# One-word key selection, with the larger tile compared in bfloat16 on VectorE and its ones summed by ScalarE

## The chip, the cores and the metric

One core of one Trainium2 chip runs one inference step of a small decoder: two layers, a prompt of 1024 tokens and a group of 8 x 8 sampled tokens. The metric is the device time of one execution in microseconds (us), the median over the runs shown. Engines are named as in the profile: PE is TensorE, DVE is VectorE, ACT is ScalarE, POOL is GpSimd, SP is SyncE.

## What is computed

Layer 0 is an RWKV-7 mixer, layer 1 an attention whose keys are chosen by an indexer; each is followed by a feed-forward block. The change lies in the choice of keys of layer 1. For each query the 256 best scored keys are kept:

```
score = einsum('bths,bth->bts', relu(logits), wi)        # 8 index heads, added up with weights
adm   = pos_k <= pos_q
_, idx = top_k(where(adm, score, -inf), 256)             # ties: the lower position first
o     = softmax over the 256 chosen keys only, then the values
```

The kernel doesn't sort. It finds, for every query (one query per partition), the 256th largest score as a threshold, by bisection over the 31 bits below the sign, and then turns the row of scores into a mask that is added to the attention logits.

## The kernel before, in words

The prompt is split in group A (64 sampled tokens and 512 prompt tokens) and group B (512 prompt tokens). Most of the work is a float32 product split in three matmuls of high and low parts (`mm3`, line 140); its inputs are weights that SP loads, ACT rounds (line 122, `wh`), and POOL or DVE subtracts (line 126, `wl`). Results are added to the residual stream by DVE (lines 388, 392, 394, tiles `xr` and `rt`).

Attention of A is written in `att_mixed`, of B in `att_prompt`. In both, Python generators are advanced in turn by `together`, one step of each per round, and a share of a step of a background generator (`side`: the output projection and feed-forward block of the other group) is drawn per round at a rate from a table. The tile framework then sets the final order on each engine: it lists the instructions by readiness under its own estimates of their length, so the order on PE, DVE and ACT moves wherever these estimates move. Each engine takes its own list strictly in order.

A tile of prompt queries has its scores computed by `att_post` (lines 1140 to 1151: matmuls `ip`, ACT's `rl`, DVE's sum into `sc`), its threshold found by `topk`, and is then attended in `att_tile` (line 1264: logits plus mask, DVE; line 1268: exponential, ACT; lines 1285 to 1291: transposes and values, PE). `topk` runs four times:

- on tiles 3 and 4 of A together (384 and 512 keys), beside tiles 1 and 2 of A and the index scores of the sampled tokens;
- on the sampled tokens alone (64 partitions, 2056 keys), beside tiles 3 and 4 of A;
- on tiles 0 and 1 of B together (640 and 768 keys), beside the scores of tiles 2 and 3;
- on tiles 2 and 3 of B together (896 and 1024 keys), beside tiles 0 and 1.

Everything in `topk` is on DVE. Line 1190 copies the upper halves of the float32 words to bfloat16 tiles `tu`. Line 1197 (`count`) compares a row with a threshold per partition and adds up the ones in the same instruction (`accum_out`, which shows as a second instruction, a read of the accumulator). Per bit there are six instructions for a pair of tiles and five for the sampled tokens: line 1204 sets the bit in the candidate (`tcand`), line 1205 turns it into a float (`tcf`, for negative thresholds with all bits flipped by `txm`), line 1197 counts each tile (from `tu` for bits 30 to 16, from `sc` below), line 1207 asks whether 256 or more passed (`tok`), and line 1208 keeps the candidate where so (`tm`). After the last bit one more count gives the number above the threshold, and lines 1224 to 1232 make the mask.

Of the kernel before, what the change touches and what calls it, by code (L numbers as in the profile page):

```python
# [9 lines left out]
F32 = mybir.dt.float32  # L10
F32R = mybir.dt.float32r
F16 = mybir.dt.float16
I32 = mybir.dt.int32
BF16 = mybir.dt.bfloat16
AF = mybir.ActivationFunctionType
ALU = mybir.AluOpType
# [9 lines left out]
TOPK = 256  # L26
# [51 lines left out]
class Kern:  # L78
# [1092 lines left out]
    def topk(self, pp, scs, R=128, place={}, order=None):  # L1171

        nc = self.nc
        n = len(scs)
        def T1(nm, shape, dt=F32):
            tag, bufs = place.get(nm, (nm, 1))
            return pp.tile(shape, dt, name=nm, tag=tag, bufs=bufs)
        Lm = max(s.shape[1] for s in scs)
        cnt = T1("cnt", [128, n])[0:R]
        m = T1("tm", [128, n], I32)[0:R]  # L1180
        cand = T1("tcand", [128, n], I32)[0:R]
        cf = T1("tcf", [128, n], I32)[0:R]
        xm = T1("txm", [128, n], I32)[0:R]
        ok = T1("tok", [128, n], I32)[0:R]
        junk = T1("tj", [128, Lm], BF16)[0:R]

        ups = []
        for i, s in enumerate(scs):
            u = T1("tu%d" % i, [128, Lm], BF16)[0:R, 0:s.shape[1]]
            nc.vector.tensor_copy(u, s.bitcast(BF16).rearrange("p (l b) -> p l b", b=2)[:, :, 1])  # L1190
            ups.append(u)
        yield

        def count(th, op, src):
            for i, s in enumerate(src):
                L = s.shape[1]
                nc.vector.tensor_scalar(out=junk[:, 0:L], in0=s, scalar1=th if isinstance(th, float) else th[:, i:i + 1], scalar2=None,
                                        op0=op, op1=ALU.add, accum_out=cnt[:, i:i + 1])
        count(0.0, ALU.is_ge, scs)
        nc.vector.tensor_scalar(out=xm, in0=cnt, scalar1=float(TOPK) - 0.5, scalar2=-1.0, op0=ALU.is_lt, op1=ALU.mult)  # L1200
        nc.vector.memset(m, 0)
        yield
        for b in range(30, -1, -1):
            nc.vector.tensor_scalar(out=cand, in0=m, scalar1=1 << b, scalar2=None, op0=ALU.bitwise_or)
            nc.vector.tensor_tensor(out=cf, in0=cand, in1=xm, op=ALU.bitwise_xor)
            count(cf.bitcast(F32), ALU.is_ge, ups if b >= 16 else scs)
            nc.vector.tensor_scalar(out=ok, in0=cnt, scalar1=float(TOPK) - 0.5, scalar2=None, op0=ALU.is_ge)
            nc.vector.copy_predicated(m, ok, cand)
            yield
        nc.vector.tensor_tensor(out=cf, in0=m, in1=xm, op=ALU.bitwise_xor)  # L1210
        th = cf.bitcast(F32)
        count(th, ALU.is_gt, scs)
        yield
        for i, s in enumerate(scs):
            L = s.shape[1]
# [143 lines left out]
    def att_mixed(self):  # L1359

        nc, I, g = self.nc, self.I, GA
        LS = PAST + 8
        self.scratch("OA", [8, 128, 576])
        with ExitStack() as ctx:
            P = lambda n, b, c=ctx, **k: c.enter_context(self.tc.tile_pool(name=n, bufs=b, **k))
            pp = self.ap2 = P("atts", 1)
            T1 = lambda nm, shape, dt=F32, tag=None, bufs=None: pp.tile(shape, dt, name=nm, tag=tag or nm, bufs=bufs)
# [4 lines left out]
            csm = T1("csm", [64, 8])  # L1372
# [14 lines left out]
            with ExitStack() as c1:  # L1387
# [7 lines left out]
                with ExitStack() as c2:  # L1395
# [7 lines left out]
                p2, p3 = P("attt", 1, c1), P("attsi", 1, c1)  # L1403
                ssc = p3.tile([64, LS], F32, name="ssc")
                tiles = [None] + [self.att_tile(g, i, p2, S[i], 512) for i in range(1, 5)]
                smp = [self.sample_index(p3, ssc, gather, ki_rows, csm), self.topk(p3, [ssc], 64, {"tj": ("kis", 1), "tu0": ("rls", 1), "teq": ("kiraw", 2), "trk": ("kiraw", 2)},
                                                                                                   lambda s: [s[:, a * 1024:a * 1024 + 1024].rearrange("r (b c) -> r c b", b=2)[:, c0:c0 + 256]
                                                                                                              for a in range(2) for c0 in (0, 256)] + [s[:, PAST:LS].unsqueeze(2)])]
                self.together(RATES["tile1A"], [self.topk(p2, S[3:5], place={"teq": ("sm", 3), "trk": ("sm", 3)})], tiles[1:3], smp[0:1])
# [328 lines left out]
```

## Time and profile before

| | us |
|---|---|
| median of 3 runs | 4378.32 |
| the three runs | 4378.32, 4389.85, 4348.06 |
| the profiled execution, own time | 4376.47 |
| its span, first to last instruction | 4374.7 |
| busy: PE, DVE, ACT, POOL | 4008.7, 2647.1, 1681.9, 971.5 |

An engine's busy time is the time in which at least one of its instructions is under way. PE is busy for 92% of the span, so a time lost or gained elsewhere counts only where PE stands still or runs at a lower clock because of it. Times inside the span are counted from its first instruction.

### The profile page before, as it was taken

The numbers are of one execution on the slowest core, as the hardware profiler recorded it, in microseconds if no ns is written. First come the engines' busy times: TensorE is split into PE (matmuls) and PEld (weight loads), VectorE is DVE, ScalarE is ACT, GpSimd is POOL, SyncE is SP. The second block draws the span as 40 slices with busy tenths as digits, with TensorE's granted clock in tenths as the row PEclk, the third lists the DMA queues.
The fourth block names the chain that finished last, engine by engine and source line by source line (L and its number), as shares of the span: only waits on it lengthen the run. The fifth ranks groups of instructions, "written<-read, shape, count | busy, mean of one in ns | idle before, by whom it ended". The sixth has DMA issues, their size and how long they took to land. (4 is left out here: it accounts for less than half of the span.)

```text
span 4374.7 us, 77889 instructions
## 1 busy us (share of the span) xinstructions
PE 4008.7 (92%) x31096; PEld 3205.7 (73%) x31096; DVE 2647.1 (61%) x6822; ACT 1681.9 (38%) x3169; POOL 971.5 (22%) x762
## 2 busy tenths in 40 slices
PE   7997899998999999989899888989778999999999
PEld 5796566666777799988655565778667667998887
DVE  5513766565677655552887964442899965555444
ACT  5533544443345333332444333332443333333333
POOL 1321222222333222211111122222110000222222
PEclk7797779998798999998899999998879999999999
DMA  6675222333221122234332145444211111322332
GB/s 224 211 237 183 66 65 78 99 89 95 59 56 51 45 80 82 78 114 140 102 84 67 53 153 193 141 128 151 69 50 41 40 39 34 116 87 90 96 96 87
DMA packets 506749, 433.94 MB, mean 99 GB/s; under 512 B 93777, under 2 KB 451777, under 8 KB 501202
## 3 DMA queue, kind: packets, MB, share of 16 engines
q1 hardware_dynamic: 500498, 391.20, 30.2%
q0 software_dynamic: 5888, 37.75, 2.5%
q8 instruction: 245, 4.01, 0.4%
q14 instruction: 118, 0.97, 0.1%
HBM read 360.48 MB, written 67.87 MB: 98 GB/s over the span
## 5 line engine op out<-in xcount | busy, mean ns | idle before, releaser
L126 POOL TENSOR_TENSOR wl<-w,wh 128x1024 fp32r<-128x1024 f32 (+1 forms) x258 | 615.8, 2391 | 2330.8 <-ACT wh L122 2076.9
L140 PE MATMUL o<-hi,wh 128*128 128x512 f32 (+4 forms) x2592 | 891.8, 347 | 27.3 <-ACT hi L144 23.6
L140 PE MATMUL o<-lo,wh 128*128 128x512 f32 (+4 forms) x2592 | 890.7, 345 | 18.4 <-DVE lo L145 14.1
L140 PE MATMUL o<-hi,wl 128*128 128x512 f32 (+4 forms) x2592 | 886.3, 343 | 2.5 <-DVE wl L126 2.3
L122 ACT CAST wh<-w 128x1024 fp32r<-128x1024 f32 (+3 forms) x388 | 396.4, 1035 | 985.8 <-PE o L140 816.0
L388 DVE SCALAR_TENSOR_TENSOR xr<-o,mods,xr 128x256 f32<-128x256 f32 (+1 forms) x816 | 463.3, 570 | 292.9 <-PE o L140 281.0
L140 PEld LDWEIGHTS o<-hi,wh 128*128 128x128 f32 (+1 forms) x2592 | 499.2, 194 | 86.6 <-ACT hi L144 28.8
L140 PE MATMUL o<-uh,wh 128*128 128x320 f32 (+2 forms) x1536 | 522.1, 340 | 41.5 <-DVE xr L388 33.0
L140 PEld LDWEIGHTS o<-lo,wh 128*128 128x128 f32 (+1 forms) x2592 | 500.2, 193 | 74.2 <-DVE lo L145 20.1
L140 PEld LDWEIGHTS o<-hi,wl 128*128 128x128 f32 (+1 forms) x2592 | 499.1, 193 | 50.8 <-issue 10.0
L140 PE MATMUL o<-uh,wl 128*128 128x320 f32 (+2 forms) x1536 | 515.3, 336 | 1.8 <-POOL wl L126 1.1
L140 PE MATMUL o<-ul,wh 128*128 128x320 f32 (+2 forms) x1536 | 516.7, 336 | 0.0
L140 PEld LDWEIGHTS o<-uh,wh 128*128 128x128 f32 x1536 | 294.3, 192 | 80.3 <-DVE xr L388 41.0
L140 PEld LDWEIGHTS o<-uh,wl 128*128 128x128 f32 x1536 | 294.2, 192 | 29.8 <-issue 5.7
L140 PEld LDWEIGHTS o<-ul,wh 128*128 128x128 f32 x1536 | 294.7, 192 | 28.0 <-issue 5.8
L126 DVE TENSOR_TENSOR wl<-w,wh 128x1024 fp32r<-128x1024 f32 (+2 forms) x130 | 183.6, 1412 | 216.5 <-ACT wh L122 212.1
L145 DVE TENSOR_TENSOR ul<-z,uh 128x512 fp32r<-128x512 f32 (+1 forms) x128 | 128.5, 1004 | 164.2 <-ACT uh L144 164.1
L1018 PE MATMUL o<-wl,hi 128*128 128x256 f32 (+2 forms) x648 | 188.1, 292 | 6.9 <-POOL wl L126 6.9
L1018 PE MATMUL o<-wh,hi 128*128 128x256 f32 (+2 forms) x648 | 187.1, 291 | 6.9 <-ACT hi L144 6.9
L1018 PE MATMUL o<-wh,lo 128*128 128x256 f32 (+2 forms) x648 | 183.9, 291 | 0.0
L1268 ACT ACTIVATE sm<-sm,st 128x128 f32<-128x128 f32 (+7 forms) x128 | 99.3, 776 | 139.4 <-DVE st L1267 83.8
L1018 PEld LDWEIGHTS o<-wl,hi 128*128 128x128 f32 (+1 forms) x648 | 126.8, 196 | 9.1 <-POOL wl L126 9.1
(411 smaller groups left out, 7063.1 us busy)
## 6 DMA issues: line engine op xcount, KB each, us to landing
w<-in_w_up SPq DMA_DIRECT2D x128, 512.0 KB
w<-in_w_down SPq DMA_DIRECT2D x128, 512.0 KB
wa<-in_w_ada SPq DMA_DIRECT2D x96, 512.0 KB
w<-in_rw_w_rkv SPq DMA_DIRECT2D x48, 512.0 KB
w<-in_att_w_in SPq DMA_DIRECT2D x32, 512.0 KB
RA<-pt SPq DMA_DIRECT2D x48, 288.0 KB
RB<-pt SPq DMA_DIRECT2D x48, 256.0 KB
in<-RA SPq DMA_DIRECT2D x32, 320.0 KB
```

What stands on the lines that cost most here:

```text
L122: nc.scalar.copy(h[:kp, :n], w[:kp, :n])
L126: eng.tensor_tensor(out=l[:kp, :n], in0=w[:kp, :n], in1=h[:kp, :n], op=ALU.subtract)
L140: nc.tensor.matmul(o[0:M, 0:c1 - c0], a, b[:, c0:c1], start=(i == 0 and q == 0), stop=(i == n - 1 and q == 2))
L145: (lo_eng or self.nc.vector).tensor_tensor(out=lo, in0=src, in1=hi, op=ALU.subtract)
L388: nc.vector.scalar_tensor_tensor(out=xm[:, p0:c1], in0=o[:, p0 - c0:c1 - c0], scalar=self.mods[l][:, j * 8 + m, 8:9], in1=xm[:, p0:c1], op ...
L1018: nc.tensor.matmul(o[0:n, 0:cw], a, w, start=(k == 0 and q == 0), stop=(k == 7 and q == 2))
L1268: nc.scalar.activation(out=sm[:, 0:L], in_=sm[:, 0:L], func=AF.Exp, scale=-1.0, bias=mn[:, 0:1], accum_out=sums)
```

## The change

The threshold is kept in one word, `tcf`, instead of `tm`, `tcand` and `txm`: the bit under test is always set in it. After the counts, line 1207 makes `tno`, which is the bit's value where fewer than 256 passed and 0 elsewhere, and line 1209 takes that bit out again and sets the next one, with two exclusive-ors in one instruction. So the small instructions of a bit are two in place of four.

For pairs, only the last, larger tile still has a bfloat16 copy (`tu`). In the first 15 bits it is compared by an instruction without accumulation (line 1193, bfloat16 in, `tg` in bfloat16 out), and ACT copies `tg` onto itself and adds it up into the same column of `cnt` (line 1194). The smaller tile is counted in float32 as in the lower bits. The sampled tokens have no copy any more and are counted in float32 for all bits. Lines behind line 1190 have moved by one in the changed kernel.

```diff
-        m = T1("tm", [128, n], I32)[0:R]
-        cand = T1("tcand", [128, n], I32)[0:R]
         cf = T1("tcf", [128, n], I32)[0:R]
-        xm = T1("txm", [128, n], I32)[0:R]
-        ok = T1("tok", [128, n], I32)[0:R]
+        no = T1("tno", [128, n], I32)[0:R]
         junk = T1("tj", [128, Lm], BF16)[0:R]
-        ups = []
-        for i, s in enumerate(scs):
-            u = T1("tu%d" % i, [128, Lm], BF16)[0:R, 0:s.shape[1]]
-            nc.vector.tensor_copy(u, s.bitcast(BF16).rearrange("p (l b) -> p l b", b=2)[:, :, 1])
-            ups.append(u)
-        yield
-        def count(th, op, src):
-            for i, s in enumerate(src):
+        if n > 1:
+            last = T1("tu", [128, Lm], BF16)
+            nc.vector.tensor_copy(last, scs[-1].bitcast(BF16).rearrange("p (l b) -> p l b", b=2)[:, :, 1])
+            ge = T1("tg", [128, Lm], BF16)
+            yield
+        def count(th, op, upper=False):
+            if upper:
+                nc.vector.tensor_scalar(out=ge, in0=last, scalar1=th[:, n - 1:n], scalar2=None, op0=op)
+                nc.scalar.activation(out=ge, in_=ge, func=AF.Copy, accum_out=cnt[:, n - 1:n])
+            for i, s in enumerate(scs[:-1] if upper else scs):
                 L = s.shape[1]
                 nc.vector.tensor_scalar(out=junk[:, 0:L], in0=s, scalar1=..., scalar2=None,
                                         op0=op, op1=ALU.add, accum_out=cnt[:, i:i + 1])
...
         for b in range(30, -1, -1):
-            nc.vector.tensor_scalar(out=cand, in0=m, scalar1=1 << b, scalar2=None, op0=ALU.bitwise_or)
-            nc.vector.tensor_tensor(out=cf, in0=cand, in1=xm, op=ALU.bitwise_xor)
-            count(cf.bitcast(F32), ALU.is_ge, ups if b >= 16 else scs)
-            nc.vector.tensor_scalar(out=ok, in0=cnt, scalar1=float(TOPK) - 0.5, scalar2=None, op0=ALU.is_ge)
-            nc.vector.copy_predicated(m, ok, cand)
-            yield
+            count(th, ALU.is_ge, n > 1 and b >= 16)
+            nc.vector.tensor_scalar(out=no, in0=cnt, scalar1=float(TOPK) - 0.5, scalar2=float(1 << b), op0=ALU.is_lt, op1=ALU.mult)
+            if b:
+                nc.vector.scalar_tensor_tensor(out=cf, in0=no, scalar=1 << (b - 1), in1=cf, op0=ALU.bitwise_xor, op1=ALU.bitwise_xor)
+            else:
+                nc.vector.tensor_tensor(out=cf, in0=no, in1=cf, op=ALU.bitwise_xor)
+            yield
```

The orders below are those of the two programs, without times. On DVE, in the last of the four selections (896 and 1024 keys), one bit of the first 15 stands like this in the kernel before; `ql` and `PT` belong to the attention of tiles 0 and 1, `xr` and `rt` to the background block of group A.

```order
L1207 TENSOR_SCALAR tok<-cnt 128x2
L388 SCALAR_TENSOR_TENSOR xr<-o,mods_108,xr 128x256
L1208 COPY_PREDICATED tm<-tok,tcand 128x2
L392 TENSOR_TENSOR rt<-o,mods_108 128x64
L1204 TENSOR_SCALAR tcand<-tm 128x2
L388 SCALAR_TENSOR_TENSOR xr<-o,mods_108,xr 128x256
L1205 TENSOR_TENSOR tcf<-tcand,txm 128x2
L394 TENSOR_TENSOR xr<-xr,rt 128x64
L1197 TENSOR_SCALAR tj,cnt<-tu_37530,tcf 128x896
L388 SCALAR_TENSOR_TENSOR xr<-o,mods_108,xr 128x256
L1163 TENSOR_TENSOR ql<-qt,qh 64x512
L1197 TENSOR_SCALAR tj,cnt<-tu_37532,tcf 128x1024
```

The four small instructions are spread over the background work, and both tiles are counted in place. In the changed kernel, same engine and same selection, a bit of the first 15:

```order
L1209 SCALAR_TENSOR_TENSOR tcf<-tno,tcf 128x2
L388 SCALAR_TENSOR_TENSOR xr<-o,mods_108,xr 128x256
L1193 TENSOR_SCALAR tg<-tu,tcf 128x1024
L1197 TENSOR_SCALAR tj,cnt<-sc_35016,tcf 128x896
L394 TENSOR_TENSOR xr<-xr,rt 128x64
L388 SCALAR_TENSOR_TENSOR xr<-o,mods_108,xr 128x256
L392 TENSOR_TENSOR rt<-o,mods_108 128x64
L1288 COPY PT<-pt 128x128
L1207 TENSOR_SCALAR tno<-cnt 128x2
L394 TENSOR_TENSOR xr<-xr,rt 128x64
```

Two small instructions are gone, the 1024 wide count has become the compare of line 1193, and line 1207 now waits for ACT; whatever stands behind it in the list waits with it. Over the 45 such bits, 43 have at least one other DVE instruction between the smaller tile's count and line 1207; the mean is 3.3 of them with 512 keys, 3.4 with 768 and 5.5 with 1024.

On ACT the new sums stand among the exponentials (`sm`), the copies out of PSUM (`PT`, `z`), and the rounding of weights (`wh`). The same selection, changed kernel:

```order
L1194 ACTIVATE tg,cnt<-tg 128x1024
L1269 ACTIVATE sm,st<-sm,st 128x640
L1288 COPY PT<-pt 128x512
L1194 ACTIVATE tg,cnt<-tg 128x1024
L122 CAST wh<-w 128x1024
L1288 COPY PT<-pt 128x128
L1194 ACTIVATE tg,cnt<-tg 128x1024
L1162 CAST qh<-qt 128x512
L409 ACTIVATE z<-o 128x256
L410 ACTIVATE z<-z 128x576
L1194 ACTIVATE tg,cnt<-tg 128x1024
```

Nothing of that stood there before but the rows without line 1194. On PE no instruction is added or taken away, but the background matmuls of line 140 have moved. Counted in the two orders: from the first logits matmul of A (`sp`) to the first logits matmul of the sampled tokens (`sps`) there are 638 of them before and 582 now, and 55 more stand between there and the first index scores of B (211 and 628 before, 226 and 668 now). From the last index scores of B (`ip`) to the last logits of B there are 1154 before and 993 now, and behind that 3425 and 3587.

## Rows read from the trace of the kernel before

**Rows 1.** The profile's page: busy time and share of the span of the engines, then the busy share in tenths of PE, of DVE and the granted PE clock in 40 equal slices of the span.

```profile
PE 4008.7 (92%) x31096; PEld 3205.7 (73%) x31096; DVE 2647.1 (61%) x6822; ACT 1681.9 (38%) x3169; POOL 971.5 (22%) x762
...
PE   7997899998999999989899888989778999999999
...
DVE  5513766565677655552887964442899965555444
...
PEclk7797779998798999998899999998879999999999
```

**Rows 2.** Busy time of each engine in the stretches of the four selections, in the order of the list above (from their first to about their last bit); then the granted clock, the DMA share and rate. The last row is the sum.

```profile
2185.00:2325.00 140.00, 131.22 (x602) 75.61 (x601) 124.33 (x435) 64.08 (x160) 23.10 (x18) 0.95 0.31 82
2365.00:2530.00 165.00, 141.46 (x713) 98.93 (x712) 154.20 (x317) 51.68 (x98) 21.45 (x9) 0.92 0.18 50
3086.00:3310.00 224.00, 174.52 (x921) 145.46 (x919) 203.06 (x541) 85.56 (x156) 28.29 (x13) 0.80 0.19 58
3306.00:3511.00 205.00, 185.63 (x1178) 137.27 (x1178) 189.34 (x596) 70.36 (x140) 14.33 (x6) 0.94 0.15 39
sum 734.00, PE 632.83 PEld 457.26 DVE 670.92 ACT 271.68 POOL 87.17; mean PE 158.21 PEld 114.31 DVE 167.73 ACT 67.92 POOL 21.79
```

**Rows 3.** What PE waited for from 2790 to 3300 us: the waiting line, what it waited for, us in total, times, longest.

```profile
PE ip L1169 <- DVE ql L1163: 10.4, 6, 3.0
PE o L342 <- DVE rsAy L170: 10.2, 1, 10.2
```

**Rows 4.** The same from 3300 to 3550 us.

```profile
PE pt L1285 <- DVE PT L1287: 15.8, 10, 4.9
```

**Rows 5.** Groups of DVE instructions by line and shape: the counts of line 1197 from the bfloat16 copies (`tu`) and from float32 (`sc`); busy us and mean ns of one, then idle time before them.

```profile
L1197 DVE TENSOR_SCALAR_CACHE_REDUCE tj<-tu,tcf 128x512 bf16<-128x512 bf16 x15 | 11.1, 742 | 0.3
L1197 DVE TENSOR_SCALAR_CACHE_REDUCE tj<-tu,tcf 128x768 bf16<-128x768 bf16 x15 | 15.1, 1006 | 0.1
L1197 DVE TENSOR_SCALAR_CACHE_REDUCE tj<-tu,tcf 128x1024 bf16<-128x1024 bf16 x15 | 19.1, 1274 | 0.2
L1197 DVE TENSOR_SCALAR_CACHE_REDUCE tj<-sc,tcf 128x1024 bf16<-128x1024 f32 x17 | 21.7, 1275 | 0.2
L1197 DVE TENSOR_SCALAR_CACHE_REDUCE tj<-sc,tcf 128x384 bf16<-128x384 f32 x17 | 10.4, 610 | 0.5
L1197 DVE TENSOR_SCALAR_CACHE_REDUCE tj<-sc,tcf 128x640 bf16<-128x640 f32 x17 | 14.9, 876 | 0.3
L1197 DVE TENSOR_SCALAR_CACHE_REDUCE tj<-sc,tcf 128x896 bf16<-128x896 f32 x17 | 19.4, 1140 | 0.2
```

**Rows 6.** DVE busy time of line 1204 alone, summed over the four stretches of rows 2.

```profile
sum 734.00, DVE 22.02; mean DVE 5.50
```

**Rows 7.** The same of line 1208 alone.

```profile
sum 734.00, DVE 26.60; mean DVE 6.65
```

**Rows 8.** All instructions of lines 1204 and 1207: shortest, median and longest in ns, first and last start.

```profile
L1204 DVE TENSOR_SCALAR tcand<-tm x124: 134/165/2391, 2193.1 to 3504.1; 128x2 int32<-128x2 int32 x93, 64x1 int32<-64x1 int32 x31
L1207 DVE TENSOR_SCALAR tok<-cnt x124: 125/164/2395, 2199.9 to 3507.8; 128x2 int32<-128x2 f32 x93, 64x1 int32<-64x1 f32 x31
```

**Rows 9.** DVE in order of time in the last selection: start, duration, line and tile.

```profile
3341.72 0.17 DVE L1207 TENSOR_SCALAR tok<-cnt 128x2 int32<-128x2 f32 x1
3341.79 0.22 DVE L394 TENSOR_TENSOR xr<-xr,rt 128x64 f32<-128x64 f32 x1
3341.92 0.16 DVE L1208 COPY_PREDICATED tm<-tok,tcand 128x2 int32<-128x2 int32 x1
3341.99 0.48 DVE L388 SCALAR_TENSOR_TENSOR xr<-o,mods,xr 128x256 f32<-128x256 f32 x1
```

**Rows 10.** Compares on DVE that don't add up (line 1224, where the mask is made), float32 in and out, by shape.

```profile
L1224 DVE TENSOR_SCALAR teq<-sc,tcf 128x512 f32<-128x512 f32 x6 | 2.9, 480 | 0.0
L1224 DVE TENSOR_SCALAR teq<-sc,tcf 128x128 f32<-128x128 f32 x1 | 0.3, 286 | 0.0
```

**Rows 11.** All copies of line 1190: shortest, median and longest in ns.

```profile
L1190 DVE COPY tu<-sc x6: 356/580/2697, 2191.3 to 3260.3; 128x384 bf16<-128x384 bf16 x1, 128x512 bf16<-128x512 bf16 x1, 128x640 bf16<-128x640 bf16 x1, 128x768 bf16<-128x768 bf16 x1
L1190 DVE COPY tu<-ssc x1: 1222/1222/1222, 2368.2 to 2368.2; 64x2056 bf16<-64x2056 bf16 x1
```

**Rows 12.** Groups on ACT that add up along the row (the exponentials of line 1268) and their reading of the accumulator, by shape.

```profile
L1268 ACT ACTIVATE sm<-sm,st 128x512 f32<-128x512 f32 x16 | 11.6, 724 | 20.7 <-DVE st L1264 17.4 <-DVE tok L1207 1.4 <-DVE tcf L1205 1.3
L1268 ACT ACTIVATE sm<-sm,st 128x768 f32<-128x768 f32 x16 | 15.0, 937 | 20.2 <-DVE st L1267 18.9 <-DVE tok L1207 1.3
L1268 ACT ACTIVATE sm<-sm,st 128x896 f32<-128x896 f32 x8 | 8.3, 1044 | 23.3 <-DVE st L1267 23.2
L1268 ACT ACTIVATION_READ_ACCUMULATOR sm<-sm,st 128x1 f32 x104 | 19.6, 189 | 0.0
```

**Rows 13.** What ACT waited for from 3060 to 3310 us, the longest of its waits: us in total, times, longest.

```profile
ACT wh L122 <- PE o L140: 57.2, 9, 23.9
```

**Rows 14.** Two stretches in which PE has nothing but line 140, the first with 512 columns in each matmul (group B's), the second with 320 and 256 (group A's); columns as in rows 2.

```profile
2800.00:2850.00 50.00, 50.00 (x220) 40.84 (x219) 24.44 (x30) 15.21 (x20) 12.60 (x5) 1.00 0.32 95
3770.00:3820.00 50.00, 49.35 (x370) 48.84 (x369) 25.00 (x65) 16.55 (x24) 12.09 (x5) 1.00 0.28 80
```

**Rows 15.** All subtractions of line 126 on POOL: shortest, median and longest in ns.

```profile
L126 POOL TENSOR_TENSOR wl<-w,wh x258: 729/2402/3968, 58.0 to 4344.0; 128x1024 fp32r<-128x1024 f32 x125, 64x1024 fp32r<-64x1024 f32 x1, 32x1024 fp32r<-32x1024 f32 x1, 128x512 fp32r<-128x512 f32 x1
```

More of the change, by code (lines that the diff above doesn't have):

```diff
@@ L1198, in count @@
                                         op0=op, op1=ALU.add, accum_out=cnt[:, i:i + 1])
-        count(0.0, ALU.is_ge, scs)
-        nc.vector.tensor_scalar(out=xm, in0=cnt, scalar1=float(TOPK) - 0.5, scalar2=-1.0, op0=ALU.is_lt, op1=ALU.mult)
-        nc.vector.memset(m, 0)
+        count(0.0, ALU.is_ge)
+        nc.vector.tensor_scalar(out=no, in0=cnt, scalar1=float(TOPK) - 0.5, scalar2=-1.0, op0=ALU.is_lt, op1=ALU.mult)
+        nc.vector.tensor_scalar(out=cf, in0=no, scalar1=1 << 30, scalar2=None, op0=ALU.bitwise_xor)
+        th = cf.bitcast(F32)
         yield
         for b in range(30, -1, -1):
-            nc.vector.tensor_scalar(out=cand, in0=m, scalar1=1 << b, scalar2=None, op0=ALU.bitwise_or)
-            nc.vector.tensor_tensor(out=cf, in0=cand, in1=xm, op=ALU.bitwise_xor)
-            count(cf.bitcast(F32), ALU.is_ge, ups if b >= 16 else scs)
-            nc.vector.tensor_scalar(out=ok, in0=cnt, scalar1=float(TOPK) - 0.5, scalar2=None, op0=ALU.is_ge)
-            nc.vector.copy_predicated(m, ok, cand)
+            count(th, ALU.is_ge, n > 1 and b >= 16)
[4 more added lines that the diff above has]
+                nc.vector.tensor_tensor(out=cf, in0=no, in1=cf, op=ALU.bitwise_xor)
             yield
-        nc.vector.tensor_tensor(out=cf, in0=m, in1=xm, op=ALU.bitwise_xor)
-        th = cf.bitcast(F32)
-        count(th, ALU.is_gt, scs)
+        count(th, ALU.is_gt)
         yield
@@ L1405, in att_mixed @@
                 tiles = [None] + [self.att_tile(g, i, p2, S[i], 512) for i in range(1, 5)]
-                smp = [self.sample_index(p3, ssc, gather, ki_rows, csm), self.topk(p3, [ssc], 64, {"tj": ("kis", 1), "tu0": ("rls", 1), "teq": ("kiraw", 2), "trk": ("kiraw", 2)},
+                smp = [self.sample_index(p3, ssc, gather, ki_rows, csm), self.topk(p3, [ssc], 64, {"tj": ("kis", 1), "teq": ("kiraw", 2), "trk": ("kiraw", 2)},
                                                                                                    lambda s: [s[:, a * 1024:a * 1024 + 1024].rearrange("r (b c) -> r c b", b=2)[:, c0:c0 + 256]
```

## The prediction

> **What bounds the kernel now.** I read the page first. PE is busy for 92% of the span, and in the 40 slices it stands at 7 or 8 tenths just where DVE reaches 8 and 9: slices 20 to 24 and 29 to 33, the two attention stages, where the selections run [rows 1]. So for the whole program PE is the bound, but in these two places it is held up. The four selection stretches make that exact [rows 2]: DVE is busy for 671 of 734 us (91%), PE for 633, so PE is idle for 101 us, and its granted clock is 0.92 to 0.95 in three of them and 0.80 in the third. Idle and clock together are all that this change can win: 101 us plus 0.05 x 140 + 0.08 x 165 + 0.20 x 224 + 0.06 x 205 = 77 us.
>
> The waits of PE say why it is idle: in group B it waits for DVE's `ql`, for the end of the norm's small chain (`rsAy`, 10.2 us at one time) and for DVE's `PT` [rows 3, 4]. None of these is the selection's result; they are short DVE instructions that stand in line behind counts of about 1 us each. DVE bounds the stretches by the length of its list, and a shorter list helps in proportion.
>
> **The change part by part.**
>
> *Small instructions.* Of four per bit two go (lines 1204 and 1208), 2 x 31 in each of four selections, 248 in all; the other two are replaced one for one by instructions of the same size. Their busy time is 22.0 + 26.6 = 48.6 us [rows 6, 7], but that is too much: a neighbour that doesn't depend on them starts 0.07 us behind them, though they last 0.16 [rows 9]. Where the next one depends on them the whole 0.165 us counts [rows 8]. By the first price 248 x 0.07 = 17.4 us, by the busy time 48.6; I take the middle of 0.07 and 0.165, nearly 0.125, so 31.0 us.
>
> *Compare in place of count.* The bfloat16 count costs what the float32 count costs, 1.274 and 1.275 us for 1024 keys [rows 5], so leaving the copies of the smaller tiles and of the sampled tokens loses nothing. The larger tile's count becomes a compare without a sum. The nearest rows are the float32 compares of line 1224: 0.286 us for 128 keys and 0.480 for 512, so 0.505 ns per key more [rows 10]; worked on, 0.609 us for 768 and 0.739 for 1024. Against 0.742, 1.006 and 1.274 that saves 0.262, 0.397 and 0.535, times 15 bits: 17.9 us. Bounds: nothing, if the compare runs as slowly as the count; or every compare as short as the 128 wide one, 15 x (0.456 + 0.720 + 0.988) = 32.5 us. I take 17.9, since that row is the same operation.
>
> The Trainium skill ("VectorE: DVE Perf Modes", section on the perf-mode tier table) puts this operation at four elements a cycle in bfloat16 and two in float32. The float32 slope above agrees with two; no run here shows four. With half the slope, an estimate by that page, the saving would be 26.4 us and the sum some 8 us better.
>
> *Copies.* Three smaller copies at the median 0.58 and the one of 1.22 us go [rows 11]: 2.9 us.
>
> *The new wait.* Line 1207 now waits for ACT's sum. ACT needs 0.724 + 0.189 us for 512 keys and 0.937 + 0.189 for 768; from 768 and 896 the slope is 0.84 ns per key, so 1.15 + 0.189 for 1024 [rows 12]. DVE counts the smaller tile meanwhile: 0.610, 0.876 and 1.140 plus the reading of about 0.08. So ACT is late by 0.22, 0.17 and 0.12 us, 15 x 0.51 = 7.6 us. It is busy with other work for 37% of the stretches [rows 2]; with half a 0.8 us instruction ahead that adds 45 x 0.37 x 0.4 = 6.7 us. But in 43 of the 45 bits the order has other DVE work in front of line 1207, three to five instructions, which is enough for most of these 14 us. I take 4 us. Bounds: 0, and 47 us if each of the 45 finds a whole rounding of 1.05 us ahead of it. What stands behind line 1207 and so waits too are `xr`, `rt`, `PT` and the masked logits, for which PE waits.
>
> *POOL against DVE.* Some of the 2-column instructions took 2.39 us instead of 0.165 [rows 8], as long as POOL's subtraction (median 2.40) [rows 15]. The new compare may be stopped in the same way, the count was not. POOL is busy for 87 of 734 us [rows 2]; 45 x 0.12 x 1.2 = 6.5 us at worst. On the other side per bit only two small ones are left to be stopped, and a POOL instruction stops whichever comes first. I set the balance at 0, with 6.5 us as the bound below nothing of the compare.
>
> The Trainium skill has a rule that speaks against the change here ("SBUF — State Buffer", section on who interferes with whom): a compare without an accumulator may take the port pair shared with GpSimd and be blocked for a whole instruction, while the form with one doesn't contend. The trace agrees so far: no group of counts has a mean above its size, and the outliers are all on small instructions and copies. By the rule alone the sum would be worse by the 6.5 us.
>
> *Sum on DVE.* 31.0 + 17.9 + 2.9 - 4 = 47.8 us off the list, times the 0.914 for which DVE is the busy one: the stretches shorten by 43.7 us.
>
> *What moves behind.* That isn't the gain, for PE's work doesn't shrink. The order puts 161 background matmuls of B's stage and 41 of A's behind their stages. At PE's full pace these cost 50/370 = 0.135 us (A's shape) and 50/220 = 0.227 us each [rows 14]: 21.8 + 9.3 = 31.1 us of PE time that the end has to bear. They take DVE work with them, 25.0/370 = 0.068 and 24.4/220 = 0.111 us per matmul: 15.4 x 0.914 = 14.1 us less in the stretches. Elsewhere DVE is busy for half the time, which covers it there. Net: 43.7 + 14.1 - 31.1 = 26.7 us. SP and POOL carry the same work; their lists move only with the background steps.
>
> The profiled execution took 4376.47 us, 2 us below the median of 4378.32: 4376.5 - 26.7 = 4350 us.
>
> **The rivals.**
>
> *Faster: the clock comes back as well.* In the third stretch PE ran at 0.80, in the fourth, with fewer and shorter stops, at 0.94 [rows 2]. If shorter waits lift the third to 0.94, that is 0.14 x 224 = 31 us more: 4319. For it: the low slices coincide with the long DVE waits. Against: the order takes background matmuls out of that stretch, and they were what kept PE busy in it.
>
> *No change: only as much as was moved out.* If the stretches shorten just by the matmuls that left, 31 us, PE's idle time stays and the end takes it all back: 4376. For it: PE waits there for chains of dependent DVE instructions, whose latency a shorter list doesn't cut. Against: the 10.2 us behind `rsAy` are a chain of eleven with counts in between.
>
> *Slower: two lists in order, each waiting for the other.* Line 1207 waits for ACT, and ACT's list has roundings of weights that wait for PE to give a buffer back: 57.2 us in 9 waits, 6.4 us each, in the third stretch alone [rows 13]. A sum behind such a rounding holds up DVE, and with it the `xr` and `PT` for which PE waits. Without any wait the gain is 26.7 + 4 x 0.914 = 30.4 us, so it turns at 30.4 / (45 x 0.914) = 0.74 us of waiting per bit. If every third bit meets one, 15 x 6.4 x 0.914 = 88 us: 4376 - 30 + 88 = 4434. Against it: the order places the sums between exponentials and copies mostly, with few roundings directly ahead.
>
> *The compare isn't faster than the count.* Then 17.9 x 0.914 = 16 us are missing: 4366. It lies inside my range.
>
> **How the numbers follow.** My case, a gain of 5 to 42 us, has 0.50; the returning clock 0.26; no change 0.15, the slow compare included; the slower rival 0.09, 0.07 of it beyond 1%. About 1%, 44 us, is what a measurement of this kernel can tell from no change (the three runs lie 42 us apart). Faster by over 1% is below 4334.5: 0.26 and 0.04 from the edge of my case, 0.30. Slower 0.07, within 1% 0.63. All bounds at their best give (48.6 + 32.5 + 2.9) x 0.914 + 14.1 - 31.1 = 60 us, 4317, and with the clock 4286; all at their worst (17.4 - 6.5 + 2.9 - 47) x 0.914 + 14.1 - 31.1 = -47, 4424. The range of 8 in 10 leaves out the ends of both: 4300 to 4395.
>
> **What would show it.** Right: line 1193 at about 0.48, 0.61 and 0.74 us; DVE's busy time down by some 45 to 60 us; the four stretches shorter by 50 to 60 us together; the end with PE saturated longer by some 25; waits of line 1207 for line 1194 below 10 us. Wrong: such waits of 30 us or more, or PE's wait for `xr` and `PT` longer than before; stretches as long as before; or a clock near 0.94 in the third stretch, which would be the faster rival.

## The result, and the profile after

The changed kernel takes 4335.6 us (median of 11 runs, 4323.6 to 4353.0) against 4378.3 of the kernel before (11 runs, 4348.1 to 4402.9). The ratio is 0.9907, 95% interval [0.9885, 0.9928], so 32 to 50 us less. Forecast were 4350 and a range of 4300 to 4395. The profiled execution has a span of 4321.8 us in place of 4374.7. Its own time, 4323.6, is the shortest of the eleven and 12 us below the median, so differences read from the profiles come out larger than the gain in time.

The page of the changed kernel, busy time and the same three slice rows as [rows 1]:

```profile
PE 3985.2 (92%) x31096; PEld 3187.3 (74%) x31096; DVE 2582.2 (60%) x6521; ACT 1716.7 (40%) x3259; POOL 974.1 (23%) x762
...
PE   7997999999998999989799979989888999999999
...
DVE  5513676564677655551886964452898955555444
...
PEclk6897688997798999999799989998889999999999
```

PE has as many instructions as before and is busy for 23.5 us less: the same matmuls ran shorter, at a higher clock. Its idle time fell from 366.0 (4374.7 - 4008.7) to 336.6 us, by 29.4. These two are the 52.9 us of the span. DVE is busy for 64.9 us less.

The four selections between the same marks as [rows 2] (from about the same distance ahead of the first test against 256 to about the same distance behind the last), changed kernel, columns as there:

```profile
2183.00:2296.00 113.00, 109.83 (x542) 63.36 (x541) 97.53 (x345) 66.97 (x180) 18.68 (x15) 1.00 0.31 84
2355.00:2500.00 145.00, 125.38 (x653) 90.02 (x654) 139.03 (x247) 49.67 (x91) 21.74 (x9) 0.94 0.20 59
3055.00:3250.00 195.00, 152.13 (x831) 126.30 (x830) 178.35 (x452) 92.50 (x181) 23.72 (x11) 0.83 0.20 62
3250.00:3432.00 182.00, 170.39 (x1080) 125.04 (x1080) 162.41 (x503) 81.45 (x162) 12.79 (x5) 0.94 0.14 36
sum 635.00, PE 557.73 PEld 404.72 DVE 577.31 ACT 290.59 POOL 76.93; mean PE 139.43 PEld 101.18 DVE 144.33 ACT 72.65 POOL 19.23
```

The selections are through in 635 us in place of 734. They hold less of PE's work, though, so they don't give the gain. For that, marks are needed between which the work is the same but for the background: from the first count of A's tiles to the first logits of the sampled tokens (`sps`), and from the last output projection of the sampled tokens to B's last logits. First the kernel before, then the changed one, columns as above:

```profile
2191.90:2578.10 386.20, 341.15 (x1635) 219.33 (x1633) 323.18 (x840) 146.76 (x317) 61.47 (x40) 0.93 0.27 75
3036.20:3698.00 661.80, 578.37 (x3550) 449.09 (x3550) 538.69 (x1551) 250.43 (x470) 61.14 (x28) 0.89 0.18 53
sum 1048.00, PE 919.52 PEld 668.42 DVE 861.87 ACT 397.19 POOL 122.61; mean PE 459.76 PEld 334.21 DVE 430.93 ACT 198.60 POOL 61.30
```

```profile
2189.10:2540.40 351.30, 319.70 (x1583) 206.74 (x1581) 291.37 (x695) 152.43 (x342) 56.56 (x38) 0.96 0.28 79
3005.20:3626.00 620.80, 549.25 (x3387) 421.73 (x3387) 491.90 (x1368) 270.06 (x518) 58.14 (x26) 0.90 0.18 52
sum 972.10, PE 868.95 PEld 628.47 DVE 783.27 ACT 422.49 POOL 114.70; mean PE 434.47 PEld 314.24 DVE 391.63 ACT 211.24 POOL 57.35
```

The two attention stretches are 75.9 us shorter, with 78.6 us less of DVE and 50.6 us less of PE; PE's idle time in them is 25.3 us less. What left them shows behind: the stretch from B's last logits to the first store, before and after,

```profile
3698.00:4005.20 307.20, 293.20 (x2019) 277.13 (x2018) 174.74 (x402) 100.41 (x148) 67.74 (x28) 0.98 0.29 87
```

```profile
3626.00:3951.80 325.80, 312.16 (x2181) 296.23 (x2180) 189.23 (x430) 108.41 (x161) 72.97 (x30) 0.99 0.29 89
```

is 18.6 us longer for 162 more matmuls. Another 6.7 us went into the sampled tokens' attention (458.1 to 464.8), 0.5 into the last stretch. So from the first count to the end the gain is 75.9 - 18.6 - 6.7 - 0.5 = 50.1 us.

The groups that answer to [rows 5, 8 and 12], DVE first, then ACT:

```profile
L1207 DVE TENSOR_SCALAR tno<-cnt 128x2 int32<-128x2 f32 x93 | 24.7, 266 | 3.8 <-ACT tg L1194 2.8
...
L1209 DVE SCALAR_TENSOR_TENSOR tcf<-tno,tcf 128x2 int32<-128x2 int32 x90 | 19.4, 216 | 1.5
...
L1193 DVE TENSOR_SCALAR tg<-tu,tcf 128x1024 bf16<-128x1024 bf16 x15 | 7.2, 482 | 0.2
...
L1193 DVE TENSOR_SCALAR tg<-tu,tcf 128x768 bf16<-128x768 bf16 x15 | 6.2, 416 | 0.2
...
L1193 DVE TENSOR_SCALAR tg<-tu,tcf 128x512 bf16<-128x512 bf16 x15 | 5.3, 354 | 0.4
```

```profile
L1194 ACT ACTIVATE tg<-tg 128x1024 bf16<-128x1024 bf16 x15 | 15.8, 1055 | 4.2 <-DVE tg L1193 4.0
...
L1194 ACT ACTIVATION_READ_ACCUMULATOR tg<-tg 128x1 f32 x45 | 8.6, 191 | 0.0
```

The compare of 1024 keys takes 0.482 us, less than half the count of [rows 5], and DVE waited for ACT's sum for 2.8 us in all.

PE's waits that answer to [rows 3 and 4], changed kernel, from 2760 to 3250 and from 3250 to 3480 us:

```profile
PE o L140 <- DVE xr L388: 12.3, 3, 8.1
...
PE o L342 <- DVE rsAy L170: 6.7, 1, 6.7
PE ip L1169 <- DVE ql L1163: 5.3, 3, 3.0
```

```profile
PE sp L1168 <- DVE st L1265: 7.6, 5, 2.6
PE pt L1286 <- DVE PT L1288: 4.9, 6, 2.0
```

The waits for `ql`, `rsAy` and `PT` fell from 36.4 to 16.9 us in all. The one for `xr` grew, in the first of the two stretches from the 8.5 us of this row of the kernel before

```profile
PE o L140 <- DVE xr L388: 8.5, 2, 8.0
```

to 12.3, in the second from 0.7 to 3.3. All end, as before, with short DVE instructions.

### The profile page after: what moved, and what is told of

The parts are those of the page before. It is cut to its first block, busy times and chain, and to the rows that moved or that the text cites. A ratio compares the mean times of both kernels' runs of the same rounds, so it can differ in the third digit from the quotient of the medians.

```text
span 4321.8 us, 77710 instructions
## 1 busy us (share of the span) xinstructions
PE 3985.2 (92%) x31096; PEld 3187.3 (74%) x31096; DVE 2582.2 (60%) x6521; ACT 1716.7 (40%) x3259; POOL 974.1 (23%) x762
## 5 line engine op out<-in xcount | busy, mean ns | idle before, releaser
L140 PE MATMUL o<-hi,wh 128*128 128x512 f32 (+4 forms) x2592 | 883.5, 344 | 25.3 <-ACT hi L144 22.5
L140 PEld LDWEIGHTS o<-lo,wh 128*128 128x128 f32 (+1 forms) x2592 | 495.9, 191 | 74.9 <-DVE lo L145 20.6
L140 PEld LDWEIGHTS o<-ul,wh 128*128 128x128 f32 x1536 | 294.4, 192 | 26.4 <-issue 4.0
L1197 DVE TENSOR_SCALAR_CACHE_REDUCE tj<-sc,tcf 128x384 bf16<-128x384 f32 (+5 forms) x147 | 135.1, 919 | 1.3
```

The source lines that it names most:

```text
L140: nc.tensor.matmul(o[0:M, 0:c1 - c0], a, b[:, c0:c1], start=(i == 0 and q == 0), stop=(i == n - 1 and q == 2))
```

## The experiments

Each kernel was run beside the kernel before. In the table, "gain" (us) is the ratio's distance from 1 times 4378; diffs are against the changed kernel, and "..." marks lines left out. The other columns are of one profiled execution each: the change against the kernel before of DVE's busy time (whole span), and, from the first count of A's tiles to the end, of PE's idle and of PE's busy time; PE's instructions are the same 31096 everywhere, so less busy time is shorter matmuls. The part ahead of the first count is left out: no kernel changes it, and it alone took 2171 to 2208 us, at granted clocks of 0.89 to 0.87.

| kernel | median us | ratio, 95% interval | gain | DVE | PE idle | PE busy |
|---|---|---|---|---|---|---|
| the change | 4335.6 | 0.9907 [0.9885, 0.9928] | 41 | -64.9 | -28.4 | -21.7 |
| the change, again (e11) | 4346.5 | 0.9923 [0.9893, 0.9953] | 34 | -63.6 | -24.8 | -17.6 |
| one word alone (e1) | 4367.8 | 0.9960 [0.9933, 0.9987] | 18 | -38.5 | -17.8 | +4.6 |
| compare and sum alone (e2) | 4342.0 | 0.9895 [0.9862, 0.9928] | 46 | -29.3 | -22.5 | -15.6 |
| the same, again (e12) | 4344.7 | 0.9913 [0.9885, 0.9942] | 38 | -31.2 | -24.1 | -9.3 |
| float32 compare (e3) | 4334.4 | 0.9879 [0.9841, 0.9917] | 53 | -58.0 | -34.9 | -25.2 |
| ACT sums twice (e4) | 4344.5 | 0.9901 [0.9867, 0.9935] | 43 | -54.8 | -16.1 | -17.6 |
| matmuls put back (e5) | 4333.1 | 0.9892 [0.9843, 0.9942] | 47 | -67.9 | -22.6 | -17.3 |
| e1, put back (e6) | 4371.5 | 0.9980 [0.9954, 1.0007] | 9 | -34.5 | -11.1 | +1.4 |
| e3, more put in (e7) | 4322.9 | 0.9881 [0.9837, 0.9925] | 52 | -58.4 | -30.9 | -27.1 |
| e3, put back (e8) | 4346.5 | 0.9922 [0.9895, 0.9950] | 34 | -50.5 | -29.1 | -15.1 |
| more small ones (e9) | 4351.0 | 0.9924 [0.9899, 0.9949] | 33 | -45.8 | -22.9 | -12.7 |
| long count added (e10) | 4363.6 | 0.9963 [0.9937, 0.9990] | 16 | -31.5 | -19.2 | -5.1 |

One profile tells little of the clock, which differs from run to run, but it can be set beside all runs. In all 14 profiles PE's busy time multiplied by the run's mean granted clock lies between 3650 and 3660. So 3655 divided by a run's clock is an estimate of PE's busy time, good to some 5 us. Averaged over all runs it is 4010 us for the kernel before, 3997 for the change, 4013 to 4022 for e1, e6 and e10, and 3985 to 4011 for the other nine, with e8, e9 and e12 at 4007 to 4011. What remains of the span is idle time: 369 us before, 337 with the change, 339 in e9, 342 in e10, and 355 in e4.

**One part at a time (e1, e2).** In e1 only the arithmetic of the threshold is changed, and both tiles are counted from bfloat16 copies as before:

```diff
...
-            if upper:
-                nc.vector.tensor_scalar(out=ge, in0=last, ...)
-                nc.scalar.activation(out=ge, in_=ge, func=AF.Copy, accum_out=cnt[:, n - 1:n])
-            for i, s in enumerate(scs[:-1] if upper else scs):
+            for i, s in enumerate(ups if upper else scs):
...
```

> Only the one-word arithmetic; the counts stand as in the kernel before, from bfloat16 copies of all tiles, and ACT takes no part. Theory 1 (the stretches are bound by the length of DVE's list): DVE's busy time falls by the two small instructions per bit, 30 to 38 us of the 65 us that the whole change took off, and the time by two thirds of that, as in the whole change (42.7 of 64.9): 20 to 25 us, 4354 to 4358. Theory 2 (the chain of a bit counts, whatever DVE's sum): the chain of each bit loses two dependent instructions of 0.165 us in all four selections, 124 x 0.33 = 41 us, nearly the whole gain: 4337. Rival (the whole gain comes from the sum on ACT): below 8 us, 4370 or more.

In e2 the compare and ACT's sum are there, and `tm`, `tcand`, `txm` with the four small instructions per bit come back (the sampled tokens stay in float32):

```diff
...
+            nc.vector.tensor_scalar(out=cand, in0=m, scalar1=1 << b, scalar2=None, op0=ALU.bitwise_or)
+            nc.vector.tensor_tensor(out=cf, in0=cand, in1=xm, op=ALU.bitwise_xor)
             count(cf.bitcast(F32), ALU.is_ge, n > 1 and b >= 16)
+            nc.vector.tensor_scalar(out=ok, in0=cnt, scalar1=float(TOPK) - 0.5, scalar2=None, op0=ALU.is_ge)
+            nc.vector.copy_predicated(m, ok, cand)
...
```

> Only the compare on DVE and the sum on ACT for the larger tile; the small instructions are the four of the kernel before, the sampled tokens are counted in float32. Theory 1: DVE's busy time falls by 15 x (0.388 + 0.590 + 0.792) = 26.6 us and 2.9 us of copies, about 30 us, and the time by two thirds, 19 us: 4359. Theory 2 (the chain of a bit): the chain of a bit hardly shortens, since ACT's sum takes as long as the count it replaces; under 8 us: 4370 or more. Rival (the whole gain comes from here): 4340.

The busy times add up: 38.5 + 29.3 = 67.8 us against 64.9. The times don't follow them. The part that takes more off DVE gains 18 us [6, 29], the one that takes less 46 [32, 60]. So e1 comes near its theory 1 and rules out the 41 us of theory 2, and e2 lands on its rival (4342.0 for 4340). The two attention stretches of e1 show where its gain stays out, columns as above; e2's stand below them:

```profile
2187.00:2531.80 344.80, 305.61 (x1521) 195.09 (x1519) 287.63 (x701) 137.40 (x305) 53.84 (x38) 0.96 0.27 77
3012.30:3659.60 647.30, 571.48 (x3390) 434.32 (x3390) 513.33 (x1401) 242.93 (x458) 57.25 (x26) 0.87 0.17 50
```

```profile
2193.20:2580.00 386.80, 345.51 (x1660) 225.03 (x1658) 318.96 (x829) 159.18 (x352) 64.47 (x41) 0.93 0.27 77
3023.70:3667.40 643.70, 571.52 (x3579) 446.06 (x3579) 518.97 (x1528) 277.16 (x531) 61.85 (x28) 0.91 0.19 55
```

In e1's stretch of B PE stands idle for 75.8 us in place of 83.4, but its clock is 0.87, below the 0.89 of before and the 0.90 of the whole change. The matmuls there became longer, and the 7.6 us are gone again. e2 is another picture: its order puts 53 matmuls more into the two stretches than the kernel before has, so these shorten by 17.5 us only. Another 20.6 us are gained outside them, 14.4 of it in the sampled tokens' attention. The matmuls that left there, 21 and behind B 29, account for some 9 us at the prices of [rows 14]. The other 12 lie where no selection runs, and no run shows what they come from. Without them e2's profile still gives 0.9 us per us of DVE (26 for 29.3), e1's 0.3 (13.2 for 38.5). So a us of DVE is not worth the same in both parts; e9 and e10 below ask why.

**The compare's size (e3).** The copy goes, and the larger tile is compared from its float32 scores:

```diff
-            last = T1("tu", [128, Lm], BF16)
-            nc.vector.tensor_copy(last, scs[-1].bitcast(BF16)...)
+            last = scs[-1]
```

> The whole change, but line 1193's compare reads the float32 row itself, not a bfloat16 copy. The question is what the compare of the prediction was mis-sized by: the float32 rows gave 0.480, 0.609 and 0.739 us, measured in bfloat16 were 0.354, 0.416 and 0.482. If the type of the input sets the pace: compares at 0.48, 0.61 and 0.74 us, DVE's list 15 x (0.126 + 0.193 + 0.257) = 8.6 us longer less three copies of 0.55, so 4 us or so on the time, 4340, not to be told from the changed kernel by time, only by the trace. Rival: leaving out the accumulation alone sets the pace, and the compares stay at 0.35 to 0.48.

The compares of e3, with all 45 (shortest, median, longest) behind them:

```profile
L1192 DVE TENSOR_SCALAR tg<-sc,tcf 128x1024 bf16<-128x1024 f32 x15 | 11.2, 747 | 0.2
...
L1192 DVE TENSOR_SCALAR tg<-sc,tcf 128x768 bf16<-128x768 f32 x15 | 9.2, 616 | 0.3
```

```profile
L1192 DVE TENSOR_SCALAR tg<-sc,tcf x45: 456/620/2383, 2191.4 to 3332.2; 128x512 bf16<-128x512 f32 x15, 128x768 bf16<-128x768 f32 x15, 128x1024 bf16<-128x1024 f32 x15
```

0.747 and 0.616 us are the 0.739 and 0.609 that the prediction took from float32 rows, so the type of the input sets the pace, and the rival is out. The bfloat16 form saves another 0.265 us per compare of 1024 keys, but e3 is as fast as the whole change within its interval of ±17 us: what bfloat16 itself is worth in time can't be seen here.

**ACT's list (e4).** Each sum is made twice, the first into a spare column, so that the one that counts comes later:

```diff
+                nc.scalar.activation(out=ge, in_=ge, func=AF.Copy, accum_out=spare)
                 nc.scalar.activation(out=ge, in_=ge, func=AF.Copy, accum_out=cnt[:, n - 1:n])
```

> The whole change, but ACT makes each sum twice, first into a spare column, so that the sum of a bit comes 0.8 to 1.25 us later and ACT has 47 us more work. It prices the rival that I held for the slower side (two lists in order, each waiting for the other). Theory 1: the three to five DVE instructions in front of line 1207 cover most of it; line 1207's waits for ACT rise from 2.8 us to 10 to 20 and the time by 5 to 15 us: 4341 to 4351. Slower rival: every bit hands the delay on, 45 x 1.03 = 46 us, which takes back the whole gain: 4375 to 4385.

What line 1207 (here 1209) waited for in e4:

```profile
  ACT tg L1196: 5.2, 8
```

With 47 us more of sums on ACT (the added ones, 38 us, and their readings) the wait is 5.2 us in 8 times, less than the 10 to 20 expected; the median, 4344.5, lies in theory 1's range, and the gain within the interval of the change's. So DVE's list isn't stalled by ACT's in this kernel. PE's idle time does grow by 12 us against the change (-16.1 for -28.4 in the profiles; 355 for 337 us over all runs), and shorter matmuls make up for it. This order also keeps 175 more background matmuls in the two stretches than the change's does, so it isn't the sums alone that are compared here.

**The matmuls that moved out (e5 to e8).** A rate in the table that draws the background steps is raised, so that about 140 of the matmuls stand ahead of B's last logits again (3447 behind it, as against 3587); e6 does so in e1, e8 in e3. In e7, made from e3, `post2B` and `tile0B` become 0.3 and 0.25 (3284 behind). The edit of e5, e6 and e8:

```diff
-RATES = dict(..., post0B=0.3, post2B=0.2, tile0B=0.2, tile2B=0.2)
+RATES = dict(..., post0B=0.3, post2B=0.2, tile0B=0.3, tile2B=0.2)
```

> The whole change, with the background rate beside tiles 0 and 1 of B at 0.3 in place of 0.2: 140 of the background matmuls that the change's order had put behind B's attention stand in it again (behind it 3447, as good as the 3425 of the kernel before and not the 3587 of the change). Theory (moved matmuls are paid back at the end, and were most of what the one-word arithmetic alone did not gain): 140 x 0.135 = 19 us fewer at the end, against 140 x 0.068 = 9.5 us of DVE work more in the stage; 4317 to 4327. Rival (the stage grows by all that comes in, wherever it stands): 4336.

> Only the one-word arithmetic, as in the first experiment (4368), with the same rate of 0.3: behind B's attention 3447 background matmuls, not 3584. Theory (the first experiment's gain of 14 us was what was left after 159 moved matmuls, 21 us): 9 to 19 us come back, 4349 to 4359. Rival (its small instructions were worth little in the first place): 4368, with the stage longer by what came in.

> The change with the float32 compare (third experiment, 4334), and more background work in B's attention than the kernel before had: rates 0.3 beside the scores of tiles 2 and 3 and 0.25 beside tiles 0 and 1; 3284 matmuls behind it. Theory: 303 x 0.135 = 41 us fewer at the end, 303 x 0.068 = 21 us of DVE work more in the stage; if DVE still decides there, 20 us better: 4314. Rival (PE is full there, nothing is left to fill): 4334.

> The change with the float32 compare and the rate of 0.3 beside tiles 0 and 1, 3447 matmuls behind B's attention. Like the first of these four, 9 to 19 us under the 4334 of the third experiment: 4315 to 4325; if the stage grows by all that comes in, 4334. It says whether the first of the four repeats on a neighbouring order.

The attention stretches of e5, to be read against those of the changed kernel:

```profile
2194.40:2551.10 356.70, 320.71 (x1583) 206.66 (x1581) 292.15 (x695) 152.52 (x342) 56.53 (x38) 0.95 0.28 77
3019.00:3655.50 636.50, 565.93 (x3527) 438.36 (x3527) 500.82 (x1385) 278.72 (x530) 62.08 (x28) 0.90 0.19 54
```

B's stretch holds 140 matmuls more and is 15.7 us longer; what lies behind is 14.0 us shorter. PE's idle time there stays at 71 us. So a background matmul costs its 0.11 us in the attention stage as it does behind it (0.10): it doesn't fill the gaps. That is the rival of e5. e6 and e8 ended above their rivals, e7 between its theory and its rival. None of e5, e6 and e8 is faster than the kernel that it changes; e7 has the best median of all, 4322.9, but its interval overlaps that of the change and of e3, so it isn't shown to be better.

**Small against long instructions (e9, e10).** With the parts unlike in worth, the question was whether DVE's time counts as such or only in long instructions. Both add DVE work to the changed kernel whose result nobody reads: e9 eight independent two-column instructions in each of the 45 upper bits, e10 one accumulating count of the larger tile.

```diff
+                for k in range(8):
+                    nc.vector.tensor_scalar(out=spare[:, 2 * k:2 * k + 2], in0=cf, scalar1=1, scalar2=None, op0=ALU.bitwise_or)
```

```diff
+                nc.vector.tensor_scalar(out=junk, in0=last, scalar1=th[:, n - 1:n], scalar2=None, op0=op, op1=ALU.add, accum_out=spare)
```

> The changed kernel with eight more two-column instructions on VectorE in each of the 45 upper bits of the pairs, 360 in all, which write to spare columns that nobody reads. By the busy time of such an instruction that is up to 360 x 0.16 = 58 us, by the time between two starts 360 x 0.07 = 25 us. Matmuls behind B's last logits stay at 3587. Theory 1 (what counts is the sum of VectorE's list in these stretches, 0.77 us per us as for the whole change): 25 to 45 us x 0.77 give 4355 to 4370. Theory 2 (what counts is the long instruction in front of a short one that TensorE waits for; tiny ones are squeezed into the gaps): 4330 to 4345, TensorE idle no longer than in the changed kernel by more than 10 us.

> The changed kernel with one more accumulating count of the larger tile in each of the 45 upper bits of the pairs, into a spare column that nobody reads: 15 x (0.742 + 1.006 + 1.274) = 45 us more on VectorE, in long instructions. 3547 matmuls stand behind B's last logits, 40 fewer than in the changed kernel. Theory 1 (sum of the list, 0.77 us per us): 4335.6 + 35 = 4370. Theory 2 (long instructions hold up TensorE, as the compare in place of the count gained 38 us for 29 us of VectorE): 4336 + 45 x 1.3 = 4394, most of it in B's two stretches, and clearly longer than the kernel with tiny instructions. If neither this nor that one is slower than 4345, VectorE's time in these stretches isn't what the change gained by.

The added group of e9, then one of e10's three:

```profile
L1196 DVE TENSOR_SCALAR tsp<-tcf 128x2 int32<-128x2 int32 x360 | 38.2, 177 | 0.0
```

```profile
L1195 DVE TENSOR_SCALAR_CACHE_REDUCE tj<-tu,tcf 128x1024 bf16<-128x1024 bf16 x15 | 19.1, 1271 | 0.0
```

By ratios, the 38.2 us of small ones cost 7 us (33 left of 41), with an interval that overlaps the change's; the 45.2 us of long counts (19.1 + 15.0 + 11.1) cost 25 (16 left of 41), with one that doesn't. By the medians both are somewhat dearer (15 and 28 us). By the means of their 11 and 12 runs the two differ by 18 us, give or take 9. So e10 is clearly longer than e9, as theory 2 had it, but its 4363.6 is nearer to theory 1's 4370 than to theory 2's 4394, and e9's 4351.0 lies between the two theories. The small ones cost less in good part because half of them lies beside other DVE work: they raised DVE's busy time by 19.1 us (2582.2 to 2601.3), the long counts by 33.4 (to 2615.6). Per us of that the medians give 0.81 and 0.84. That a us of DVE's busy time in short instructions is worth less is therefore not shown by this pair. e10's attention stretches:

```profile
2205.60:2563.80 358.20, 325.17 (x1590) 207.65 (x1588) 298.96 (x726) 152.09 (x343) 56.42 (x38) 0.95 0.28 77
3025.00:3673.90 648.90, 565.59 (x3428) 435.10 (x3428) 523.49 (x1440) 271.92 (x520) 59.66 (x27) 0.88 0.18 51
```

B's is 28.1 us longer than in the changed kernel; PE is idle for 83.3 us there, as before the change. With the long count back, e10 stands where e1 stands in time (16 and 18 us gained), though ACT still sums. Over all runs e10's PE is busy for 15 us longer than e9's by the estimate above (4022 and 4007) and idle for 3 us longer, so most of the 18 us between them is longer matmuls.

**What one word adds to the compare (e11, e12).** The change and e2 once more, both on one chip, to narrow this term:

> The changed kernel once more, on the same chip and in the same rounds as the kernel with the compare and ScalarE's sum alone, to see what the one-word arithmetic adds to it. Measured so far: ratio 0.9907 for the whole change, 0.9895 [0.9862, 0.9928] without the one-word arithmetic, which can't be told apart. Theory 1 (sum of VectorE's list, 0.63 us per us: 40.7 us for 64.9): the whole is 0.63 x 35.6 = 22 us shorter than the kernel without the one-word arithmetic, ratios 0.990 and 0.995. Theory 2 (the long counts decide, small instructions hardly): both within 10 us of each other, ratios 0.989 to 0.992.

> The compare in bfloat16 with ScalarE's sum, and the four small instructions per bit of the kernel before; the sampled tokens are counted in float32. Theory 1: ratio about 0.995, 4358. Theory 2: 0.989 to 0.992, 4330 to 4345. In between, 0.992 to 0.994, the one-word arithmetic is worth 5 to 15 us on top of the compare.

4346.5 and 4344.7, ratios 0.9923 and 0.9913: no difference, as theory 2 had it, and not the 22 us of theory 1. The means of the six runs of each differ by 1 us, give or take 12. On top of the compare the one-word arithmetic isn't shown to be worth anything, though it takes 32.4 us off DVE's busy time (63.6 against 31.2).

## Why the prediction was right, and where not

*What bounds the kernel.* Right in the place: the gain of the change is PE's idle time and clock in the attention stretches, and nothing was gained outside them. (The slices alone don't carry this: PE also stands at 9 in slices 21, 22, 32 and 33, and at 8 in 25 and 27, where DVE is at 4 [rows 1]. The stretches of [rows 2] do.) "A shorter list helps in proportion" held for the stretches as a whole: 0.914 us per us of DVE was forecast, and the two attention stretches are 75.9 us shorter for 78.6 us of DVE, 0.97; e1's are 55.9 shorter for 60.9, 0.92. It did not hold for the parts. e2's stretches give 17.5 us for 23.9, 0.73, and in time, once the moved matmuls are paid, one word alone gave 18 us for 38.5 of DVE, nothing measurable for 32.4 on top of the compare, and compare and sum 46 and 38 for 29.3 and 31.2. So one price for every us of DVE is the step that failed. The forecast came near partly by luck: in time it had one word too large, the compare too small, and the moved matmuls at a loss that e5 doesn't show.

*Small instructions.* Sized at 31.0 us of DVE, 28.3 in time. (The middle of 0.07 and 0.165 is 0.1175, which makes 29.1 us.) Their four lines had 102.7 us of busy time in the stretches of [rows 2], the two now have 59.0 in the new ones, so 43.7 went. In time they gave 18 us alone and nothing measurable on top of the compare. The term was too small for DVE's list and too large for the time. The prediction's own first price, 0.07 us where the next instruction doesn't depend on it, 17.4 us in all, was the nearer one.

*Compare in place of count.* The mis-sized term. Taken from float32 rows it was 17.9 us; measured are 0.482, 0.416 and 0.354, that is 15 x (0.792 + 0.590 + 0.388) = 26.6 us. The trace agrees with the 26.4 that the prediction estimated beside it by the Trainium skill ("VectorE: DVE Perf Modes", section on the perf-mode tier table). In time compare and sum alone gave 38 and 46 us, more than what they took off DVE (about as much without the part gained where no selection runs), where the forecast had 16.4 less the wait's 3.7. PE's busy time tells what the forecast's sum left out. In the profiles every kernel whose upper bits no longer count the larger tile has 9 to 27 us less of it, and e1, e6 and e10, which count it, have -5 to +5. e10's execution ran slowly from the start (2205.6 us to the first count), but e8, e9 and e12 did so as well (2204.6 to 2208.3) and have -9.3 to -15.1. Over all runs the two groups also stand apart, 3985 to 4011 us and 4013 to 4022, but e8, e9 and e12 lie within 4 us of the kernel before's 4010, so it can't be said of each kernel. That long counts in front of what PE waits for are what keeps its clock down is argued and not shown: the smaller tile's counts and those of the lower bits stand in all kernels, and a test that holds the clock and lets the waits change wasn't made.

*The new wait.* Right: 2.8 us for 4, and below 10 as said.

*POOL against DVE.* Right in its balance: of 45 bfloat16 compares none took longer than 0.490 us, while line 1207 and line 1209 still have outliers of 2.32 and 2.35. In e3 one float32 compare took 2.383 us, about POOL's subtraction of [rows 15]. The rule of the Trainium skill that speaks against the change ("SBUF — State Buffer", section on who interferes with whom) would have the bfloat16 compare blocked like that too. In this kernel's trace it was not; in e9's it was, once, beside a subtraction of POOL (start and duration in us):

```profile
2230.10 2.79 DVE L1194 TENSOR_SCALAR tg<-tu,tcf 128x512 bf16<-128x512 bf16 x1
```

```profile
2230.36 2.36 POOL L126 TENSOR_TENSOR wl<-w,wh 128x1024 fp32r<-128x1024 f32 x1
```

In the other seven kernels with a bfloat16 compare none took longer than 0.490 us. So the trace agrees that such a compare can be blocked for as long as a subtraction of POOL lasts. It happened to one compare in 360, at some 2.4 us, where the prediction's bound was 6.5 us.

*What moves behind.* The bill was 31.1 us, 25.8 came (18.6 + 0.5 behind B, 6.7 in the sampled tokens' attention). What the stretches save by it was put at 14.1 us. e5 puts it at about the bill itself, 15.7 us for 14.0, so the net of -17 us was about 0; that is shown for 140 matmuls of B's stretch, not for those of A. With compare and sum at 38 to 46, one word at little or nothing beside them and this at 0 in place of -17, the sum comes to about the measured 41 where 26.7 were forecast.

*The rivals.* The clock of the third stretch went from 0.80 to 0.83, not to 0.94, so the faster rival as it was put didn't come. The clock did rise in small steps, 0.93 to 0.96 and 0.89 to 0.90 over the two attention stretches and 0.95 to 0.96 between them, and PE was busy for 21.7 us less by it in this execution, of the 50.1. "No change" is out: PE's idle time went down by 28 us. So is the slower one: DVE waited 2.8 us for ACT, and 5.2 in e4. The slow compare is refuted by its row.

*What would show it.* Compare at 0.48, 0.61 and 0.74: wrong, 0.35 to 0.48. DVE down by 45 to 60: 64.9, more. The four stretches shorter by 50 to 60: 99 by the marks of [rows 2], 76 over the two attention stretches, more as well. The end longer by some 25: 19.1. Waits for line 1194 below 10: 2.8. Of the signs of being wrong half of one came: PE waited longer for `xr` (9.2 before, 15.6 after, over the stretches of [rows 3 and 4] and those that answer to them), and shorter for `PT` (15.8 and 4.9).

Open is why the parts don't add up in time: 18 and 38 to 46 us alone, 34 to 41 together, with intervals of ±9 to ±14 us. Every edit also gives the three engines another order, and an effect of the order of that size, such as e2's 12 us, can't be told from the edit here.

## What to carry to other kernels

A us off an engine that only holds up the bounding one isn't worth a fixed part of a us. Here taking out the long counts gave about the time that it took off DVE or more, and taking out short ones, which partly lie beside others, gave half of theirs or nothing. Price the two apart, and ask which instructions stand in front of those that the bounding engine waits for. Background work drawn out of a stage is neither a gain nor a loss where it cost its full time in there, as in e5. When a row of the trace has the same operation in another type, use it as an end of the range and not as the value.

## What was not expected of the hardware

- A compare without accumulation from bfloat16 to bfloat16 took 0.482 us for 128x1024, from float32 0.747; with accumulation both types took 1.27 [rows 5].
- Ahead of the first selection all kernels are alike, and the profiled executions still differ there by up to 37 us (2171 to 2208), at granted clocks of 0.89 to 0.87. The scatter between runs of one kernel goes with the clock too: the fastest run of the change (4323.6) has 0.916, the slowest (4353.0) 0.908. How much of it arises in this part no run shows.
- 360 small instructions of 38.2 us busy time raised DVE's busy time by 19.1 (2582.2 to 2601.3), so half of it lies beside other DVE instructions.
- ACT waited for a buffer of PE before rounding weights in 57.2 us of the third stretch [rows 13], 14.6 in the changed kernel, so the queue that the slower rival rested on had mostly gone in the new order.
